# Score matmuls of a hybrid attention trunk: 128 rows with zeros in place of 64 rows

## The chip, the cores and the metric

The kernel runs on one core of one Trainium2 chip. The metric is device time in microseconds (us) of one execution; lower is better. Three runs of the kernel before gave 862.95, 865.4 and 859.62 us, a median of 862.95. The profile was taken in one further execution.

## The reference, cut to what matters

Two layers over 256 positions of width 1024. Each layer has a mixer with three branches (sliding-window attention, a gated short convolution, block attention), gated and merged, then a SwiGLU feed-forward part; each of the two is followed by a residual and a layer norm. With 256 positions and blocks of 256, the block attention is plain causal attention. Both attentions have 8 heads of 64 channels, and their scores are the part that the change touches:

```python
# sliding window (SWA), window 128, 8 query heads on 2 key heads, with sinks
logits = einsum('bnqhgd,bnkhd->bnhgqk', q, k) * 64 ** -0.5 - slope * dist
# block attention (MoBA), here the own block alone, 8 heads
lo = einsum('bhqd,bhkd->bhqk', q, kown) * 64 ** -0.5
lo = where(dist_own >= 0, lo - slope * dist_own, -inf)
```

All of it is float32. The kernel gets this precision on TensorE by splitting each operand in a high half (rounded to the matmul's format) and a low half (what is left): a product is high*high + high*low + low*high.

## The kernel before, in words

**The weights.** The weights come as a list of 140 pieces of 128 x 2048 floats, 70 for each layer, in the order in which they are used. `load` (L143) brings a piece into one of three raw buffers by SP's queue. `split_piece` (L187) cuts it in two chunks of 1024 columns: ScalarE writes the high half `wh` (L184), VectorE the low half `wl` (L185), into a ring of four slots. TensorE uses a piece in 48 matmuls of 256 columns (or their equal), two of them with `wh` and one with `wl` for each product. All matmuls but transposes and the mixing of values are issued by the helper `mm` (L255, so the trace has L256).

**The order of the work.** The program is unrolled and its order on each engine is written out when it is built: `Plan` (L52) keeps a model time of TensorE (`T.pe`), and tasks for ScalarE and VectorE are put in their queues when that time has passed their ready time. `mm` adds to the model time by the number of columns of the moving operand alone (L257, L103). Each engine then runs its own queue in order and waits on semaphores where it needs another's result.

**The attention.** Heads are taken in pairs, a pair being one round. A layer has eight rounds: four of SWA (`swa`, L653) and four of MoBA (`moba`, L658); in this text they are r0 to r7. Rounds are woven into the weight matmuls by `tick` (L223). A round goes through these steps:

- `prepare` (L404): for each head a of the pair, `me` is the 64 partitions of the head and `other` the other 64. The query tile `xq[:, a]` gets the query's high half on `me` and its low half on `other` (L409). The key tile `xk` is `kx` of L649, with two planes for each head: plane 0 has the key's high half on `me` and a copy of the key on `other` (L412), plane 1 has the key's low half on `me`. Before the first round of a layer GpSimd writes zeros to columns 0 to 127 of plane 1 on `other` (L651).
- `scores` (L449): for each head three matmuls into one PSUM tile `s` of four blocks of 128 columns. The first (L453) takes queries 128 to 255 on all 128 rows with plane 0: high*key_high plus low*key in one pass. The second (L454) adds high*key_low for the same queries, on the 64 rows of `me` alone. The third (L455) takes queries 0 to 127 with the first 128 keys of both planes at once, on all 128 rows, into blocks 0 and 3.
- `soft` (L419): VectorE adds the distances and takes the maximum (L444 to L426), ScalarE takes the exponential (L429, L431), VectorE scales (L439 to L441). The tile is `prob`.
- `turned` (L462): TensorE transposes `prob` into `tp` (L271), ScalarE copies it to `pt` (L280).
- `mixed` (L470): TensorE multiplies `pt` with the values into `yp` (L474, L476), and ScalarE and VectorE write the two halves of `y`.

The scores of the next round follow right behind the `yp` of this one. The tile `xa` that holds `xq` and `kx` shares its place in memory ("z") with the layer-norm constants `gb` of the part before.

**The convolution** runs beside rounds r1 to r4: its taps are on GpSimd (L714 to L717), between two products on VectorE (L283).

Of the kernel before, what the change touches and what calls it, by code (L numbers as in the profile page):

```python
# [9 lines left out]
FT = mybir.dt.float32  # L10
# [6 lines left out]
P = 128  # L17
D = 1024
S = 256
# [4 lines left out]
HD = 64  # L24
# [78 lines left out]
def pe_time(cols):  # L103
    return cols / 2400 + 0.0067


def dve(n):
    return "V", 0.07 + n * 0.00104
# [7 lines left out]
def trunk(ctx: ExitStack, tc: tile.TileContext, x, xt, w, sinks, conv, ln, out):  # L116
    nc = tc.nc
# [99 lines left out]
    def later(task, fn):  # L217
        waiting.append((task, fn))
# [27 lines left out]
    def bank(shape, tag, name):  # L246

        t = ps.tile(shape, FT, tag=tag, name=name)
        if len(banks[tag]) >= 4:
            for task in banks[tag].pop(0):  # L250
                T.finish(task)
        banks[tag].append([])
        return t, banks[tag][-1]

    def mm(acc, a, b, start, stop):  # L255
        nc.tensor.matmul(acc, a, b, start=start, stop=stop)  # L256
        T.pe += pe_time(int(np.prod(b.shape[1:])))  # L257
# [10 lines left out]
    def turn(src, n):  # L268
        tp, users = bank([P, n, P], "o", "tp")
        for i in range(n):  # L270
            nc.tensor.transpose(tp[:, i, :], src(i), ident)  # L271
            T.pe += pe_time(2 * P)
        return tp, users

    def halve(dst, src, n):
        return [act(n) + (lambda: nc.scalar.activation(dst[0], src, AF.Copy),),  # L276
                dve(n) + (lambda: nc.vector.tensor_sub(dst[1], src, dst[0].bitcast(FT)),)]  # L277

    def copy(dst, src, n):
        return [act(n) + (lambda: nc.scalar.activation(dst, src, AF.Copy),)]  # L280
# [16 lines left out]
    def after(users, ops, needs=(), **k):  # L297
        t = T.add(ops, needs=list(needs) + [had for _, _, had in claims if had], **k)
        for ring, i, _ in claims:
            ring[i] = t  # L300
        claims.clear()
        users.append(t)
        return t
# [3 lines left out]
    xk = [xx[:, k] for k in range(KD)]  # L307
# [107 lines left out]
    def attend(q, k, new_k, xq, xk, v, vsel, far, slopes, sink, dst, when):  # L415
        los = [slice(a * HD, (a + 1) * HD) for a in range(2)]
        pr, pts, tasks = [], [], []

        def soft(a, st, t, s):  # L419
            def top():  # L420
                nc.vector.tensor_reduce(st[:, 0:1], t[:, 0, :], axis=AX.X, op=OP.max)
                nc.vector.tensor_reduce(st[:, 1:2], t[:, 1:3, :], axis=AX.XY, op=OP.max)
                if sink is not None:
                    nc.vector.tensor_scalar(st[:, 2:4], st[:, 0:2], sink[1][a], -0.125, op0=OP.max, op1=OP.mult)
                else:
                    nc.vector.tensor_scalar_mul(st[:, 2:4], st[:, 0:2], -0.125)  # L426

            def power():
                nc.scalar.activation(t[:, 0, :], t[:, 0, :], AF.Exp, bias=st[:, 2:3], scale=0.125,  # L429
                                     accum_out=st[:, 4:5])  # L430
                nc.scalar.activation(t[:, 1:3, :], t[:, 1:3, :], AF.Exp, bias=st[:, 3:4], scale=0.125,  # L431
                                     accum_out=st[:, 5:6])
                if sink is not None:
                    nc.scalar.activation(st[:, 6:8], st[:, 2:4], AF.Exp, bias=sink[0][a], scale=1.0)

            def scale():
                if sink is not None:
                    nc.vector.tensor_add(st[:, 4:6], st[:, 4:6], st[:, 6:8])
                nc.vector.reciprocal(st[:, 6:8], st[:, 4:6])  # L439
                nc.vector.tensor_scalar_mul(t[:, 0, :], t[:, 0, :], st[:, 6:7])  # L440
                nc.vector.tensor_scalar_mul(t[:, 1:3, :], t[:, 1:3, :], st[:, 7:8])  # L441

            return [
                dve(384) + (lambda: nc.vector.scalar_tensor_tensor(t, far, -8.0 * slopes[a], s[:, 0:3, :],  # L444
                                                                   op0=OP.mult, op1=OP.add),),
                dve(P) + (lambda: nc.vector.tensor_add(t[:, 0, :], t[:, 0, :], s[:, 3, :]),),
                ("V", 0.75, top), ("A", 1.1, power), ("V", 0.9, scale)]

        def scores():  # L449
            ss = [bank([P, 4, P], "o", "s") for a in range(2)]  # L450
            for a in range(2):
                s, me = ss[a][0], los[a]
                mm(s[:, 1:3, :], xq[:, a, P:S], xk[:, a, 0, :], True, False)  # L453
                mm(s[:, 1:3, :], xq[me, a, P:S], xk[me, a, 1, :], False, True)  # L454
                mm(s[:, 0::3, :], xq[:, a, 0:P], xk[:, a, :, 0:P], True, True)  # L455
            for a in range(2):
                st = work.tile([P, 8], FT, name="st", bufs=4)
                pr.append(work.tile([P, 3, P], FT, tag="prob", name="prob", bufs=4))
                tasks.append(after(ss[a][1], soft(a, st, pr[a], ss[a][0])))
            later(tasks[-1], turned)  # L460

        def turned():  # L462
            T.finish(*tasks)
            for a in range(2):
                tp, users = turn(lambda i: pr[a][:, i, :], 3)
                pts.append(work.tile([P, 3, P], FT, name="pt"))
                tasks.append(after(users, copy(pts[a], tp, 384)))
            later(tasks[-1], mixed)

        def mixed():  # L470
            T.finish(*tasks)
            yp, users = bank([P, S], "o", "yp")
            for a in range(2):
                nc.tensor.matmul(yp[los[a], :], v[:, 0, vsel[a]], pts[a][:, 0:2, :], start=True, stop=False)  # L474
            for a in range(2):
                nc.tensor.matmul(yp[los[a], P:S], v[:, 1, vsel[a]], pts[a][:, 2, :], start=False, stop=True)  # L476
            T.pe += pe_time(4 * 384)
            at["y"].append(after(users, halve(dst, yp, S), due=8.0))
            busy[0] -= 1

        rounds.append(Round(when, q, k, new_k, xq, xk, scores))

    def residual(acc, users, r, stats):
# [150 lines left out]
    for l in range(L):  # L634
# [13 lines left out]
        xa = keep.tile([P, 6, S], FR, tag="z", name="xa")  # L648
        xq, kx = xa[:, 0:2], xa[:, 2:6].rearrange("p (a i) s -> p a i s", a=2)  # L649
        for a in range(2):  # L650
            nc.gpsimd.memset(kx[HD - a * HD:P - a * HD, a, 1, 0:P].bitcast(FT), 0.0)  # L651

        def swa(j):  # L653
            attend(aq[:, j, :], ak, j == 0, xq, kx, av, (slice(0, HD), slice(HD, P)), far_w, (slope(j), slope(j + 4)),
# [278 lines left out]
```

## Time and profile before

| | |
|---|---|
| median of 3 runs | 862.95 us (859.62 to 865.4) |
| the profiled execution's own time | 860.16 us |
| its span, first to last instruction | 858.4 us |
| mean granted clock of TensorE | 0.997 |
| TensorE busy | 844.8 us, 98% of the span |
| VectorE, ScalarE, GpSimd busy | 68%, 53%, 6% |
| moved by DMA | 155.16 MB, 181 GB/s over the span |

The span is 1.8 us shorter than the execution's own time; that rest lies around the program. PE is TensorE's matmuls, PEld its weight loads, DVE is VectorE, ACT is ScalarE, POOL is GpSimd, SP is the engine that issues most transfers. L256 is line 256 of the kernel before. A matmul's length in a row holds its way through the array, so that matmuls overlap in the rows; what one costs is seen from the start of one to the start of the next. In a row `out<-in` are the program's tile names, then come the shape of the weights (64*128 is 64 rows and 128 columns) and the shape of the moving operand.

### The profile page before, as it was taken

The numbers are of one execution on the slowest core, as the hardware profiler recorded it, in microseconds if no ns is written. First come the engines' busy times: TensorE is split into PE (matmuls) and PEld (weight loads), VectorE is DVE, ScalarE is ACT, GpSimd is POOL, SyncE is SP. The second block draws the span as 40 slices with busy tenths as digits, with TensorE's granted clock in tenths as the row PEclk, the third lists the DMA queues.
The fourth block names the chain that finished last, engine by engine and source line by source line (L and its number), as shares of the span: only waits on it lengthen the run. The fifth ranks groups of instructions, "written<-read, shape, count | busy, mean of one in ns | idle before, by whom it ended". The sixth has DMA issues, their size and how long they took to land.

```text
span 858.4 us, 15516 instructions
## 1 busy us (share of the span) xinstructions
PE 844.8 (98%) x6374; PEld 797.3 (93%) x6374; DVE 583.5 (68%) x977; ACT 456.3 (53%) x809; POOL 51.4 (6%) x81
## 2 busy tenths in 40 slices
PE   7999999999999999999999999999999999999996
PEld 7989999999899999988899899999997999999885
DVE  5678888567976666545656798876689575666435
ACT  6667577745535445434337757776564254444320
POOL 2003400000100000000000034000000000000000
PEclk9999999999999999999999999999999999999998
DMA  8754535365755555556337352544557465555511
GB/s 300 289 195 150 187 108 186 140 216 176 265 197 180 174 187 197 196 189 238 119 116 255 116 196 99 186 138 169 196 197 254 139 245 187 173 185 193 196 50 49
DMA packets 24822, 155.16 MB, mean 181 GB/s; under 512 B 2704, under 2 KB 4528, under 8 KB 7344
## 3 DMA queue, kind: packets, MB, share of 16 engines
q1 hardware_dynamic: 23536, 149.96, 49.9%
q0 software_dynamic: 1216, 4.22, 1.5%
q8 instruction: 50, 0.82, 0.4%
q14 instruction: 20, 0.16, 0.1%
HBM read 153.11 MB, written 1.05 MB: 180 GB/s over the span
## 4 chain that ended last, share of the span: by engine, by line
PE 96%; DMA 2%; DVE 1%; ACT 0%; issue 0%; SPq 0%; POOLq 0%; POOL 0%; DVEq 0%
PE acc L256 47%; PE pr L256 17%; PE hp L256 9%; PE br L256 8%; PE gc L256 5%; PE s L256 3%; PE cv L256 3%; PE tp L271 2%; DMA gb<-ln 1%; PE yp L474 1%; DMA xs<-xt 1%; PE yp L476 0%; DVE xtok L502 0%; DVE wA L185 0%; SPq L156 0%
## 5 line engine op out<-in xcount | busy, mean ns | idle before, releaser
L256 PE MATMUL acc<-xx,wh 128*128 128x256 f32 x2304 | 408.9, 282 | 5.6 <-ACT wh L276 5.6
L185 DVE TENSOR_TENSOR wl<-raw,wh 128x1024 fp32r<-128x1024 f32 x266 | 321.9, 1228 | 123.2 <-ACT wh L184 122.3
L184 ACT ACTIVATE wh<-raw 128x1024 fp32r<-128x1024 f32 x266 | 273.5, 1054 | 188.5 <-PE acc L256 81.6
L256 PEld LDWEIGHTS acc<-xx,wh 128*128 128x128 f32 x2304 | 353.9, 190 | 6.7 <-ACT wh L276 6.2
L256 PE MATMUL acc<-xx,wl 128*128 128x256 f32 x1152 | 323.2, 281 | 0.0
L256 PEld LDWEIGHTS acc<-xx,wl 128*128 128x128 f32 x1152 | 217.7, 189 | 0.2 <-DVE wl L277 0.2
L256 PE MATMUL hp<-wh,xx 128*128 128x256 f32 x384 | 70.5, 281 | 0.0
L283 DVE TENSOR_TENSOR g<-g,acc 128x256 f32<-128x256 f32 x72 | 30.1, 417 | 58.7 <-PE acc L256 58.7
L256 PE MATMUL br<-y,wh 128*128 128x256 f32 x384 | 67.9, 281 | 0.0
L256 PE MATMUL pr<-wh,hidA 128*128 128x512 f32 (+1 forms) x216 | 60.8, 366 | 0.0
L256 PEld LDWEIGHTS hp<-wh,xx 128*128 128x128 f32 x384 | 59.5, 188 | 0.0
L256 PEld LDWEIGHTS br<-y,wh 128*128 128x128 f32 x384 | 59.0, 190 | 0.0
L256 PE MATMUL br<-y,wl 128*128 128x256 f32 x192 | 54.0, 281 | 0.0
L256 PE MATMUL hp<-wl,xx 128*128 128x256 f32 x192 | 53.5, 279 | 0.0
L256 PE MATMUL gc<-xx,wh 128*128 128x256 f32 x256 | 45.3, 281 | 0.0
L256 PEld LDWEIGHTS pr<-wh,hidA 128*128 128x128 f32 x216 | 39.1, 189 | 6.7
L256 PE MATMUL pr<-wh,hidB 128*128 128x512 f32 (+1 forms) x144 | 41.8, 366 | 0.0
L256 PE MATMUL pr<-wl,hidA 128*128 128x512 f32 (+1 forms) x108 | 39.6, 366 | 0.0
L256 PEld LDWEIGHTS gc<-xx,wh 128*128 128x128 f32 x256 | 39.3, 190 | 0.0
L429 ACT ACTIVATE prob<-prob,st 128x128 f32<-128x128 f32 x32 | 12.6, 395 | 46.3 <-DVE st L426 23.3
L256 PEld LDWEIGHTS hp<-wl,xx 128*128 128x128 f32 x192 | 36.1, 188 | 0.0
L256 PEld LDWEIGHTS br<-y,wl 128*128 128x128 f32 x192 | 36.0, 188 | 0.0
(130 smaller groups left out, 982.0 us busy)
## 6 DMA issues: line engine op xcount, KB each, us to landing
raw<-w SPq DMA_DIRECT2D x136, 1024.0 KB, 4.9
gb<-ln POOLq DMA_DIRECT2D x8, 512.0 KB, 5.9
raw<-w SPq DMA_DIRECT2D x6, 512.0 KB, 6.5
xtok<-x SPq DMA_DIRECT2D x2, 512.0 KB, 6.3
xs<-xt SPq DMA_DIRECT2D x3, 256.0 KB, 5.4
raw<-w SPq DMA_DIRECT2D x3, 256.0 KB, 5.5
out<-xtok SPq DMA_DIRECT2D x3, 256.0 KB, 2.0
xs<-xt SPq DMA_DIRECT2D x2, 128.0 KB, 2.5
```

Source lines behind the costliest of these rows:

```text
L184: return [act(n) + (lambda: nc.scalar.activation(wh[:, s], raw[j][:, s], AF.Copy),), dve(n) + (lambda: nc.vector.tensor_sub(wl[:, s], raw[ ...
L185: dve(n) + (lambda: nc.vector.tensor_sub(wl[:, s], raw[j][:, s], wh[:, s].bitcast(FT)),)]
L256: nc.tensor.matmul(acc, a, b, start=start, stop=stop)
L271: nc.tensor.transpose(tp[:, i, :], src(i), ident)
L283: return [dve(n) + (lambda: nc.vector.tensor_mul(dst, a, b),)]
L429: nc.scalar.activation(t[:, 0, :], t[:, 0, :], AF.Exp, bias=st[:, 2:3], scale=0.125, accum_out=st[:, 4:5])
L474: nc.tensor.matmul(yp[los[a], :], v[:, 0, vsel[a]], pts[a][:, 0:2, :], start=True, stop=False)
```

## The change

The second score matmul takes all 128 rows of `xq` and of plane 1 in place of the 64 rows of `me`. On the rows of `other` plane 1 has to be zero for all 256 columns, so the memset writes 256 columns in place of 128. Nothing else differs.

```diff
@@ -449,9 +449,9 @@
         def scores():
             ss = [bank([P, 4, P], "o", "s") for a in range(2)]
             for a in range(2):
-                s, me = ss[a][0], los[a]
+                s = ss[a][0]
                 mm(s[:, 1:3, :], xq[:, a, P:S], xk[:, a, 0, :], True, False)
-                mm(s[:, 1:3, :], xq[me, a, P:S], xk[me, a, 1, :], False, True)
+                mm(s[:, 1:3, :], xq[:, a, P:S], xk[:, a, 1, :], False, True)
                 mm(s[:, 0::3, :], xq[:, a, 0:P], xk[:, a, :, 0:P], True, True)
@@ -648,7 +648,7 @@
         for a in range(2):
-            nc.gpsimd.memset(kx[HD - a * HD:P - a * HD, a, 1, 0:P].bitcast(FT), 0.0)
+            nc.gpsimd.memset(kx[HD - a * HD:P - a * HD, a, 1, :].bitcast(FT), 0.0)
```

## Rows read from the trace of the kernel before

**Rows 1.** The page: busy times of the engines, TensorE's clock in 40 slices.
```profile
PE 844.8 (98%) x6374; PEld 797.3 (93%) x6374; DVE 583.5 (68%) x977; ACT 456.3 (53%) x809; POOL 51.4 (6%) x81
...
PEclk9999999999999999999999999999999999999998
```

**Rows 2.** The page: the chain that ended last, by engine.
```profile
PE 96%; DMA 2%; DVE 1%; ACT 0%; issue 0%; SPq 0%; POOLq 0%; POOL 0%; DVEq 0%
```

**Rows 3.** Waits of TensorE's matmuls: us in total, times, longest.
```profile
PE acc L256 <- ACT wh L276: 5.6, 3, 4.7
PE tp L271 <- DVE xtok L502: 0.7, 1, 0.7
```

**Rows 4.** Timeline, TensorE, round r0: start, length; each row begins one matmul later.
```profile
46.35 0.28 PE L256 MATMUL s<-xa 128*128 128x256 f32 x1
...
46.56 0.69 PE L256 MATMUL s<-xa 64*128 64x256 f32 x2
...
46.87 0.50 PE L256 MATMUL s<-xa 128*128 128x256 f32 x2
...
47.09 0.59 PE L256 MATMUL s<-xa 128*128 128x256 f32 x2
...
47.83 0.28 PE L256 MATMUL acc<-xx,wh 128*128 128x256 f32 x1
```

**Rows 5.** Timeline, TensorE's weight loads, the same round.
```profile
46.56 0.18 PEld L256 LDWEIGHTS s<-xa 64*128 64x128 f32 x1
...
46.98 0.19 PEld L256 LDWEIGHTS s<-xa 128*128 128x128 f32 x1
```

**Rows 6.** Timeline, TensorE, round r1: its six score matmuls and what follows them.
```profile
60.39 1.75 PE L256 MATMUL s<-xa 128*128 128x256 f32 x6
61.98 0.40 PE L256 MATMUL cv<-wh,xx 128*128 128x512 f32 x1
```

**Rows 7.** The chain in order of time: start, us, what.
```profile
76.24 8.18 PE acc L256 x72
...
428.99 8.48 PE hp L256 x72
```

**Rows 8.** Groups by shape: count, then busy us and mean ns of one.
```profile
L256 PE MATMUL s<-xa 64*128 64x256 f32 x32 | 12.1, 380 | 0.0
```

**Rows 9.** Stretches r3, r4: us; busy PE, PEld, DVE, ACT, POOL; clock, DMA, GB/s.
```profile
88.54:102.90 14.36, 14.36 (x119) 13.40 (x117) 13.32 (x30) 9.86 (x25) 5.02 (x4) 1.00 0.46 165
102.90:117.06 14.16, 14.16 (x119) 13.35 (x117) 10.93 (x28) 9.26 (x24) 5.18 (x7) 1.00 0.32 123
```

**Rows 10.** Timeline, VectorE: the softmax of r2 (second head), r3, r4, r5 begins.
```profile
76.27 0.56 DVE L444 SCALAR_TENSOR_TENSOR prob<-far_w,s 128x384 f32<-128x384 f32 x1 [0.19 <-PE s L256]
...
89.81 1.07 DVE L444 SCALAR_TENSOR_TENSOR prob<-far_w,s 128x384 f32<-128x384 f32 x2
...
106.21 1.00 DVE L444 SCALAR_TENSOR_TENSOR prob<-far_c,s 128x384 f32<-128x384 f32 x2
...
119.73 1.01 DVE L444 SCALAR_TENSOR_TENSOR prob<-far_c,s 128x384 f32<-128x384 f32 x2
```

**Rows 11.** Timelines, ScalarE's `pt` and TensorE's `yp` in r4, then in r5.
```profile
115.36 0.85 ACT L280 ACTIVATE pt<-tp 128x384 f32<-128x384 f32 x2
...
116.15 0.76 PE L474 MATMUL yp<-pt,mix 128*64 128x256 f32 x4
...
128.77 0.86 ACT L280 ACTIVATE pt<-tp 128x384 f32<-128x384 f32 x2
...
130.30 0.65 PE L474 MATMUL yp<-pt,mix 128*64 128x256 f32 x4
```

**Rows 12.** Timeline, GpSimd: memsets of layer 0 (one of two), layer 1.
```profile
12.55 0.20 POOL L651 MEMSET xa<- 64x128 f32 x1 [7.85 <-DMA raw<-w]
...
435.64 0.45 POOL L651 MEMSET xa<- 64x128 f32 x2 [1.69 <-DVE xtok L502]
```

**Rows 13.** The span's end, TensorE: us, busy, granted clock, DMA share, GB/s.
```profile
850.00:858.40 8.40, 1.07 (x9) 0.71 0.17 62
```

## The prediction

> **What bounds the kernel now.** I read the page first. TensorE is busy for 98% of the span at the full clock [rows 1], and 96% of the chain that ended last runs through it [rows 2]. A busy TensorE may still stand still between matmuls, so the next view is its waits: 6.3 us in all, at the first weights and at one layer norm, and none at scores, transposes or `yp` [rows 3]. So the time is TensorE's own sequence, and what a matmul of it costs is the distance of starts in the timeline.
>
> In ordinary stretches that is 8.18 / 72 = 0.114 us for a matmul of 256 columns, and 8.48 / 72 = 0.118 us where the moving operand is two blocks of 128 apart from each other, as in `hp` [rows 7]. Now the scores of round r0 [rows 4]: from the first (128 rows) to the second (64 rows) 0.21 us, from the second to the third 0.31, from the third to the next head's first 0.22; the second head repeats it and the six take 47.83 - 46.35 = 1.48 us. Six ordinary ones would take 4 x 0.114 + 2 x 0.118 = 0.69.
>
> The weight loads say why [rows 5]. In an ordinary stretch the load for the next matmul runs beside the matmul before. The load of the 64-row matmul begins only at 46.56, with the matmul itself, and that of the third begins with its matmul too, at 46.87; the fourth's begins at 46.98, ahead of its matmul at 47.09. So TensorE lets the array run empty (0.21 - 0.11 = 0.10 us) when it goes from 128 rows to 64 and again on the way back (0.10), and each time it then has a load that nothing hides (0.11 in the second's 0.31, 0.11 in the third's 0.22): 0.4 us a head.
>
> **The change part by part.**
>
> *The second matmul gets 128 rows* (32 of them [rows 8]). The columns stay at 256, so its own work stays at 0.114. Both switches of height go. In r0 the saving is 1.48 - 0.69 = 0.79 us. In the other rounds the scores follow `yp`, whose weights are 64 columns wide; the first score then has a load of its own that nothing hides, and the six take 61.98 - 60.39 = 1.59 us [rows 6]. That load stays: 0.69 + 0.11 = 0.80, and the saving is 0.79 again. Sixteen rounds give 12.6 us on TensorE.
>
> The third matmul is the one term that no row settles alone: its output goes to two blocks apart from each other, and part of its 0.22 could be that. If all of it were, 0.22 - 0.118 = 0.10 would stay for each head, 32 x 0.10 = 3.3 us, and the gain of TensorE is 9.3. The other end is 12.6. I take 12.6, since the fourth's load begins a plain 0.11 after the third's start [rows 5], and the distance is then that of a load and a matmul in line.
>
> The Trainium skill speaks against the change at one place ("TensorE: Matmul & The Clock Gate", Part 3: Packing small matmuls): matmuls on different row groups of the array run at the same time, so that a half-height one beside another costs a few ns, which full height gives up. By that rule a 64-row matmul would be nearly free and each of the 32 new ones would cost 0.114 more, 3.6 us. Here the trace does not agree: the two heads' 64-row matmuls have two full ones between them, and each has 0.31 us to itself.
>
> *The waits.* The second matmul now reads the low half of the queries, the whole of plane 1 and so the memset. The first one already waits for all of `xq`, and the third for the zeros in columns 0 to 127. Nothing new is late. One more semaphore wait could be set on the second; at 0 if it is met, as the waits of the other scores are. Behind it stands TensorE's whole queue, and the softmax waits for it; but the zeros would have to be over 30 us late to hold it (next paragraph).
>
> *The memset* doubles its columns: 0.20 us becomes 0.20 to 0.40 (an estimate, at most double), twice in each layer. On GpSimd's queue it stands ahead of `far_w` and the sinks in layer 0, at 12.55, with nothing that needs them before 47.6; in layer 1 at 435.6 with the scores at 467 [rows 12]. Cover of over 30 us: 0. No transfer is added or moved.
>
> *The order* of all queues stays, since the model time counts columns alone.
>
> *What is late next.* TensorE comes 0.79 us earlier at each round, and this is worth something only if VectorE and ScalarE follow. They feed it twice a round: `prob` for the transposes, `pt` for `yp`. Up to r2 VectorE waits for the scores, so it follows (the second softmax of r2 waits 0.19 us for TensorE [rows 10]). From then on it doesn't: in r3 VectorE is busy for 13.32 of 14.36 us [rows 9]. The start of a softmax lies 89.81 - 88.54 = 1.27 us behind the scores in r3, 3.31 in r4, 2.67 in r5 [rows 9, 10]. So r4 is where VectorE is furthest behind already, and there `pt` is done at 115.36 + 0.85 = 116.21, when `yp` has just begun at 116.15 (its second head needs the second `pt`): no room is left [rows 11].
>
> So I follow VectorE through it. It is moved by r2's scores, the third round: its two softmaxes come 2.0 and 2.4 us earlier, in line 2.2 to 2.4; I take 2.3. From there to r4's `pt` it and ScalarE work without leaning on TensorE, and r4's `pt` is done 2.3 us earlier. TensorE would be at r4's `yp` after five rounds of scores, 5 x 0.79 = 3.95 earlier. It has to wait about 3.95 - 2.35 = 1.6 us there. In r5 `pt` ends at 129.63, 0.67 before `yp` [rows 11]; VectorE's round from r4 to r5 takes 13.52 us and TensorE's new one 14.16 - 0.79 = 13.37, so it can't catch up, and TensorE is 2.35 + 0.79 = 3.14 earlier against 2.3: that uses up the room of r5 and asks for 0.1 us at the most. For r6 and r7 I take r5's room as the measure. Behind the wait three rounds still give 3 x 0.79 = 2.37.
>
> Sum for a layer: 2.35 + 2.37 = 4.7 us; layer 1 has the same order. Two layers: 9.4 us, of the 12.6 that TensorE saves; 3.2 are given back at r4.
>
> Against the profiled execution: 860.16 - 9.4 = 850.8 us. That execution lies 2.8 us under the median of the runs (862.95) and near their lowest; by the median it is 853.5. I predict between the two, 852.0.
>
> **The rivals.**
>
> *The others keep up.* VectorE and ScalarE follow TensorE wholly (their queues hold splits of weights that could be done sooner), no wait shows at r4, and all 12.6 us come through: 847.5 by the profile, 850.3 by the median. For it: the chain has 0% of either engine now [rows 2]. Against it: 13.32 of 14.36 us busy, and queues that run in order.
>
> *The third matmul keeps its 0.22*: 0.59 us a round. Five rounds are 2.95, VectorE moves by about 1.7, so 1.2 are given back a layer, and the gain is 2 x (8 x 0.59 - 1.2) = 7.0: 853.1 by the profile, 855.9 by the median. Against it stands the place of the loads.
>
> *The change doesn't do what it says*: the 0.21 and 0.31 come not from the height but from a matmul that adds to what the one before has just written, or from the semaphores on these loads. Then nothing changes, 863. Against it: `acc` and `hp` add to one tile at 0.114 throughout.
>
> *Half-height matmuls were nearly free.* If a 64-row matmul ran beside its neighbours and the distances of r0 belonged to something else that stays, each full-height one would add 0.114 us, 32 x 0.114 = 3.6: 863.8. Against it: the second score has 0.31 us to itself [rows 4]. This is what the Trainium skill's rule above would do here.
>
> *Slower, by the clock.* The wait at r4's `yp` is the one place where the change makes TensorE stand still. At the end of the span, where TensorE is busy for 1.07 of 8.4 us, its granted clock is 0.71 on the mean, so it falls towards its lower level (1.2 of 2.4 GHz) when TensorE is idle [rows 13]. If the wait of 1.6 us did that, the matmuls behind it would take twice as long until it rose again. The gain is gone when 4.7 us of matmul work a layer run at the lower level; with 10 us of it the time is 850.8 + 20 = 871. Against it: the clock is at full in every slice before the end [rows 1].
>
> **How the numbers follow.** Forecast (gain partly given back at r4) 0.57; others keep up 0.22; third matmul keeps its cost 0.12; nothing saved 0.06; half-height ones free 0.01; slower by the clock 0.02. The range goes from 846 (all 12.6 against the profile's own time, less 1.5 for a run as low as the lowest shown) to 857 (the third matmul's case by the median, and 1 more): what it leaves out is the case with nothing saved, the free half-height matmuls, the clock, and the edges of the others. What a measurement can tell from no change is about 1%, 8.6 us. My forecast of 9.4 is just over it: I give two thirds of its chance to faster, all of "keep up" and a tenth of the third matmul's: 0.38 + 0.22 + 0.01 = 0.61. Slower by over 1% is the clock's 0.02, and within 1% the rest, 0.37.
>
> **What would show it.** No weight load of 64 rows is left. Starts of the second and third score 0.11 to 0.12 after the one before; the six in 0.80 behind `yp` and 0.69 in r0 and its like in layer 1. A score group with 64 rows gone and 96 of 128. If the third still takes 0.22, that term was wrong. In r4 of each layer a wait of TensorE for ScalarE's `pt` of 1 to 2 us, and the rounds r5 to r7 shorter by 0.79. If no wait for `pt` shows, the give-back was wrong; if the waits show at the transposes, I had the wrong place. The prediction is wrong as a whole if the six scores still take 1.5 us, or if the stretch r0 to r7 is shorter by 0.79 x 8 and the time is not.

## The result, and the profile after

The kernel after took 853.75 us in the median of 4 runs (852.73 to 855.76), the kernel before 864.17 in the median of 4 (859.62 to 866.96). The ratio on record is 0.991, with a 95% interval from 0.9887 to 0.9932; the quotient of these two medians is 0.988, just below that interval. So the gain is 7.8 us by the ratio and 10.4 by the medians. The forecast was 852.0 in a range from 846 to 857. The profiled execution of the kernel after took 852.73 us with a span of 851.0, against 860.16 and 858.4 before: 7.4 us between the two profiles, where the forecast's sum was 9.4.

First the score matmuls. The groups by shape of the kernel after (count, then busy us and mean ns of one) and TensorE's timeline of rounds r0 and r1 answer to [rows 8], [rows 4] and [rows 6]:

```profile
L256 PE MATMUL s<-xa 128*128 128x256 f32 x96 | 15.4, 296 | 0.0
...
46.83 0.87 PE L256 MATMUL s<-xa 128*128 128x256 f32 x6
47.53 0.40 PE L256 MATMUL acc<-xx,wh 128*128 128x256 f32 x2
...
60.08 0.98 PE L256 MATMUL s<-xa 128*128 128x256 f32 x6
60.90 0.39 PE L256 MATMUL cv<-wh,xx 128*128 128x512 f32 x1
```

No 64-row form is left. The six scores take 47.53 - 46.83 = 0.70 us in r0 and 60.90 - 60.08 = 0.82 in r1, where it was 1.48 and 1.59. Added up over the 16 rounds, the distances of starts come to 12.8 us in place of 25.2: TensorE's own saving is 12.4 us, and the forecast had 12.6.

Now what TensorE waits for, in the kernel after (us in total, times, longest), against [rows 3]:

```profile
PE acc L256 <- ACT wh L276: 4.9, 2, 4.4
PE yp L474 <- ACT pt L280: 3.2, 3, 1.5
PE tp L271 <- DVE xtok L502: 0.9, 1, 0.9
PE acc L256 <- DVE wl L185: 0.7, 1, 0.7
```

The second row is new: `yp` waits for ScalarE's `pt`. The timelines of round r4 show where, ScalarE's row first, then TensorE's; they answer to the first pair of [rows 11]:

```profile
114.15 0.85 ACT L280 ACTIVATE pt<-tp 128x384 f32<-128x384 f32 x2
...
112.86 0.28 PE L256 MATMUL acc<-xx,wl 128*128 128x256 f32 x1
114.67 0.81 PE L474 MATMUL yp<-pt,mix 128*64 128x256 f32 x3 [1.54 <-ACT pt L280]
```

In the kernel before, the last matmul ahead of the `yp` at 116.15 was this:

```profile
115.94 0.28 PE L256 MATMUL acc<-xx,wl 128*128 128x256 f32 x1
```

After the change the last matmul ahead begins at 112.86 and `yp` at 114.67; before, that distance was 116.15 - 115.94 = 0.21 us. So the wait that came with the change is 1.81 - 0.21 = 1.60 us; in layer 1 it is 1.73 - 0.21 = 1.52. The stretch of r4 is longer than before although its scores are shorter: 15.41 us in the windows of the kernel after, against 14.16 in [rows 9] (columns as there).

```profile
86.67:100.44 13.77, 13.72 (x118) 13.06 (x116) 12.81 (x31) 10.46 (x26) 3.76 (x3) 1.00 0.46 159
100.44:115.85 15.41, 13.87 (x118) 13.08 (x117) 12.18 (x29) 9.37 (x25) 6.35 (x8) 1.00 0.35 129
```

To see what becomes of the saving I take the stretch of a layer from its first score to its first `br`, in which nothing but rounds and their weight matmuls lies, and add up TensorE's distances from start to start by what the matmul is (the one ahead of a round's transposes is counted with them). In us, for layer 0 and layer 1:

| part of the stretch | before | after | difference |
|---|---|---|---|
| scores | 12.60, 12.60 | 6.42, 6.41 | -6.2, -6.2 |
| last matmul ahead of `yp`, to `yp` | 1.77, 1.77 | 3.49, 3.53 | +1.7, +1.8 |
| `yp` | 6.51, 6.52 | 7.40, 7.41 | +0.9, +0.9 |
| transposes | 5.63, 5.63 | 5.77, 5.77 | +0.1, +0.1 |
| weight matmuls (`acc`, `cv`) | 89.59, 89.59 | 88.96, 89.05 | -0.6, -0.5 |
| all | 116.10, 116.10 | 112.04, 112.16 | -4.1, -3.9 |

So 6.2 us a layer are saved, 2.8 given back at `yp` and the transposes, and 0.6 come from somewhere that the forecast did not have (the pace of TensorE, below). By rounds, the 2.8 of layer 0 are 2.0 in r4 (1.60 ahead of `yp`, 0.28 within it, 0.14 at the transposes), 0.5 in r3 and 0.25 in r5 and r6.

Within `yp` the two heads part. In the kernel before the first matmul of the second head starts 0.01 us after that of the first in r3; in the kernel after it starts 0.38 us after it in r3 and in r4, since its own `pt` is not there, and `yp` takes 1.18 us in place of 0.80 and 0.90.

The two layers gain 8.0; ahead of the first score the kernel after happened to be 0.5 us later (46.83 against 46.35), and that leaves the 7.4 of the profiles.

### The profile page after: what moved, and what is told of

It is laid out like the page before. It is cut to its first block, busy times and chain, and to the rows that moved or that the text cites. A ratio compares the mean times of both kernels' runs of the same rounds, so it can differ in the third digit from the quotient of the medians.

```text
span 851.0 us, 15520 instructions
## 1 busy us (share of the span) xinstructions
PE 834.0 (98%) x6374; PEld 793.2 (93%) x6374; DVE 584.0 (69%) x977; ACT 455.8 (54%) x809; POOL 52.0 (6%) x81
## 4 chain that ended last, share of the span: by engine, by line
PE 88%; DVE 4%; ACT 3%; DMA 2%; POOL 2%; issue 1%; SPq 1%; POOLq 0%; DVEq 0%; ACTq 0%
PE acc L256 41%; PE pr L256 18%; PE hp L256 9%; PE br L256 8%; PE gc L256 5%; PE cv L256 3%; PE tp L271 2%; PE s L256 1%; DMA gb<-ln 1%; PE yp L474 1%; DMA raw<-w 1%; DVE wl L185 1%; ACT wh L184 1%; POOL hh L716 1%; POOL t L717 1%
## 5 line engine op out<-in xcount | busy, mean ns | idle before, releaser
L429 ACT ACTIVATE prob<-prob,st 128x128 f32<-128x128 f32 x32 | 12.6, 395 | 45.3 <-DVE st L426 23.3
```

## The experiments

All ran against the kernel before on the same chip; a ratio is the estimate on record from all runs of both kernels, with its 95% interval, and lies within 0.002 of the quotient of their medians. A trace shows one execution alone. The totals carry two things that have nothing to do with the change. The first score began between 46.2 and 48.4 us in the ten profiles of this study, and the wait of the first matmuls behind a layer norm for its constants (`tp` for `xtok`) was 0.7 to 4.6 us. So the stretch above is read beside each ratio.

### Two half-height matmuls side by side

The kernel before, with the order of the six scores changed:

```diff
-            for a in range(2):
-                s, me = ss[a][0], los[a]
-                mm(s[:, 1:3, :], xq[:, a, P:S], xk[:, a, 0, :], True, False)
-                mm(s[:, 1:3, :], xq[me, a, P:S], xk[me, a, 1, :], False, True)
-                mm(s[:, 0::3, :], xq[:, a, 0:P], xk[:, a, :, 0:P], True, True)
+            for a in range(2):
+                mm(ss[a][0][:, 1:3, :], xq[:, a, P:S], xk[:, a, 0, :], True, False)
+            for a in range(2):
+                me = los[a]
+                mm(ss[a][0][:, 1:3, :], xq[me, a, P:S], xk[me, a, 1, :], False, True)
+            for a in range(2):
+                mm(ss[a][0][:, 0::3, :], xq[:, a, 0:P], xk[:, a, :, 0:P], True, True)
```

> The kernel before with its score matmuls in another order: both heads' first ones, then both heads' 64-row ones side by side (they lie on different rows of the array), then both heads' third ones. Height theory (each change of height lets the array run empty, 0.10 us, and leaves one load uncovered, 0.11): two changes a round in place of four, the six scores of r0 take about 1.09 us in place of 1.48, 16 x 0.39 = 6.3 us saved on TensorE, some of it given back at r4, 4 to 5 us in all. Rival A (the distance comes from adding to what the matmul just before has written): the 64-row ones no longer follow the matmul that wrote their tile, all distances become 0.11 to 0.12, and the six take 0.7. Rival B (two half-height matmuls on different rows run at the same time): the distance from the first 64-row one to the second is a few hundredths of a us and the six take 0.95 or less.

Ratio 0.9946 (0.9926 to 0.9965). TensorE's timeline of r0, cut so that rows begin with the half-height pair and with the third score, its weight load between them:

```profile
48.05 1.14 PE L256 MATMUL s<-xa 128*128 128x256 f32 x6
...
48.38 0.39 PE L256 MATMUL s<-xa 64*128 64x256 f32 x2
...
48.69 0.19 PEld L256 LDWEIGHTS s<-xa 128*128 128x128 f32 x1
...
48.69 0.38 PE L256 MATMUL s<-xa 128*128 128x256 f32 x1
...
49.03 0.40 PE L256 MATMUL acc<-xx,wh 128*128 128x256 f32 x2
```

The six take 49.03 - 48.05 = 0.98 us. The two half-height matmuls together cover 0.39 us, where one alone covers 0.38: they start 3 to 4 ns apart in all 16 rounds. Ahead of them stands the 0.21 of a change to 64 rows and behind them the 0.31 back, once a round now. Rival A falls, since no score here follows the matmul that wrote its tile, and the 0.21 and 0.31 are there all the same: they belong to the height. The kernel after says so from the other side: there the second score follows the one that wrote its tile and starts 0.12 us behind it. The height theory holds for the changes and had the pair wrong, which rival B had right but for a size: 0.98 where it said 0.95 or less.

This is what the Trainium skill says ("TensorE: Matmul & The Clock Gate", Part 3): matmuls on different row groups run together. The trace agrees as soon as the two are neighbours, with 3 to 4 ns between them; in the kernel before they are not, and each cost as much as the pair. What such a pair pays is in the Trainium skill as well, without a number ("TensorEngine Tiling (Array Packing)", Key Properties: a change of mode drains the array). Here it is 0.10 us for each change, and a load of 0.11 that nothing covers behind it; the rows show this delay and not what happens in the array.

The stretch falls to 113.5 and 113.8 us. The waits at `yp` of r4 are there (2.8 us in two layers), though the saving is 4.0 a layer and not 6.2.

### The change in r5 to r7 alone, and in r0 to r4 alone

The kernel after, with the rows chosen by round:

```diff
-                mm(s[:, 1:3, :], xq[:, a, P:S], xk[:, a, 1, :], False, True)
+                on = slice(0, P) if full else los[a]
+                mm(s[:, 1:3, :], xq[on, a, P:S], xk[on, a, 1, :], False, True)
```

with `full` handed in as a new argument, false in `swa` and `j > 0` in `moba` for the late rounds, true in `swa` and `j == 0` in `moba` for the early ones.

> The kernel after with the second score on 128 rows in rounds r5 to r7 alone, on 64 rows in r0 to r4. Theory (the give-back is the wait at r4's yp, because VectorE, GpSimd and ScalarE up to there do not follow TensorE): nothing is given back, no wait for pt at r4, and 2 layers x 3 rounds x 0.77 = 4.6 us come through. Rival (the give-back is spread over all rounds, a share of each): of the 7.9 us that the attention stretches gained, 3/8 come through, 3.0 us.

> The kernel after with the second score on 128 rows in rounds r0 to r4 alone, on 64 rows in r5 to r7: the other half of the run with late rounds alone. Theory (what is given back is given back at r3 and r4): TensorE's scores shorten by 5 x 0.77 = 3.9 us a layer, the wait at r4's yp is there with about 1.7 us, and of the 3.9 about 1.5 to 2 come through in the stretch from the first score to the first br, which was 116.1 us before. Rival (a like share of each round is given back): 5/8 of what the kernel after gained there net of TensorE's pace, 5/8 x 3.4 = 2.1, and the wait is smaller, about 1.

Late rounds alone: ratio 0.9895 (0.9876 to 0.9913). Early rounds alone: 0.9956 (0.9941 to 0.9972). What TensorE waits for, late first, then early:

```profile
PE acc L256 <- ACT wh L276: 5.3, 2, 4.4
PE tp L271 <- DVE xtok L503: 4.6, 2, 4.0
```

```profile
PE acc L256 <- ACT wh L276: 4.7, 2, 4.4
PE yp L475 <- ACT pt L280: 3.2, 3, 1.5
PE tp L271 <- DVE xtok L503: 1.2, 2, 0.8
```

With the late rounds alone there is no wait for `pt`. The scores of a layer are 2.3 us shorter, the stretch is 113.75 against 116.1: all of the saving comes through (0.3 us lost within `yp` and 0.3 won by weight matmuls cancel). With the early ones alone the scores are 3.9 us shorter, the wait for `pt` is the whole 3.2 us of the kernel after, and the stretch is 114.5 and 114.9: only 1.6 and 1.2 come through. The forecast for this run was 1.5 to 2, so layer 1 lies under it; the rival's 2.1, with a wait of about 1, is farther off. So the give-back is made by the scores of r0 to r4 and paid at r3 and r4, for the most part at r4, and not by each round for itself.

One thing did not fit. The late rounds should have gained 4.6 us in all, and the ratio says 9. The chain in order of time shows a difference behind the stretch; the kernel after first, then late rounds alone:

```profile
159.03 33.92 PE br L256 x288
192.95 22.61 PE gc L256 x192
```

```profile
160.16 32.64 PE br L256 x288
192.80 21.77 PE gc L256 x192
```

The same 480 matmuls take 56.53 us in one and 54.41 in the other, 0.1178 and 0.1133 us each, in both layers. 2 x 2.1 = 4.2 us of the gain in this profile have nothing to do with scores. But the same execution lost 3.7 us again behind a layer norm (waits of 4.6 in place of 0.9), and at 856.54 us it was the slowest of six, with a median of 853.46. What the five others did no trace shows, so it is likely but not shown that the pace makes up the 9. A run on the pace comes below.

### What sets r4's `pt`

Three kernels on this. In the first the taps 1 and 2 of the convolution are left out of the kernel after, so GpSimd does one operation of five for each group, and the order on the other engines stays:

```diff
                     nc.gpsimd.tensor_mul(z, up[:, i, 0:S], tap[0])
-                    for n in (1, 2):
-                        nc.gpsimd.tensor_mul(other, up[:, i, n:S + n], tap[n])
-                        nc.gpsimd.tensor_add(z, z, other)
```

> The kernel after with the convolution's taps 1 and 2 left out (one product on GpSimd in place of five operations for each of four groups); the order on all other engines is the same. Theory (in r4 the softmax stands behind a product on VectorE that waits for these taps, so GpSimd's length sets when pt is ready): the wait at r4's yp falls from 1.7 us to 0.4 or less in each layer, 2.5 to 3 us faster than the kernel after. Rival A (ScalarE's own queue, where pt stands behind a split of weights): the wait stays at 1.3 to 1.7. Rival B (VectorE is full with splits and softmax whatever GpSimd does): it stays at over 1.

Ratio 0.9868 (0.9846 to 0.989); the profiled execution was the fastest of six (847.11, median 852.4), so the stretch is what counts. There is no wait for `pt`, the part ahead of `yp` is 1.77 us as in the kernel before, and the stretch is 109.18 us in both layers, 2.9 and 3.0 less than after. Rounds r3 and r4 run at TensorE's own pace:

```profile
86.25:99.53 13.28, 13.28 (x118) 12.84 (x116) 11.98 (x30) 9.84 (x24) 3.02 (x2) 1.00 0.39 139
99.53:112.81 13.28, 13.28 (x118) 12.84 (x116) 10.97 (x29) 9.93 (x25) 0.00 (x0) 1.00 0.38 147
```

Both rivals fall: ScalarE's queue has the same order and `pt` behind the same split, and VectorE has the same instructions, though they take less time (11.98 us busy in r3 in place of 12.81). The rows of the kernel after show the path. First GpSimd in r3 and r4, then VectorE:

```profile
98.03 1.59 POOL L716 TENSOR_TENSOR hh<-mix,cw 128x256 f32<-128x256 f32 x1
99.70 1.59 POOL L717 TENSOR_TENSOR t<-t,hh 128x256 f32<-128x256 f32 x1
...
104.19 0.61 POOL L716 TENSOR_TENSOR hh<-mix,cw 128x256 f32<-128x256 f32 x1
```

```profile
97.93 1.23 DVE L185 TENSOR_TENSOR wl<-raw,wh 128x1024 fp32r<-128x1024 f32 x1
...
100.62 1.75 DVE L185 TENSOR_TENSOR wl<-raw,wh 128x1024 fp32r<-128x1024 f32 x1
...
103.70 0.42 DVE L283 TENSOR_TENSOR t<-t,acc 128x256 f32<-128x256 f32 x1 [1.32 <-POOL t L717]
...
105.01 1.01 DVE L444 SCALAR_TENSOR_TENSOR prob<-far_c,s 128x384 f32<-128x384 f32 x2
```

The same product in the kernel before:

```profile
104.90 0.42 DVE L283 TENSOR_TENSOR t<-t,acc 128x256 f32<-128x256 f32 x1 [1.31 <-POOL t L717]
```

VectorE's product at 103.70 has waited 1.32 us for the taps, and r4's softmax stands behind it in the queue. The taps are late because they run beside splits: the same operation takes 1.59 us beside them and 0.61 with no split beside it, and a split 1.75 in place of 1.23. VectorE's wait is not new: in the kernel before it was 1.31 us for the same taps. What is new is that TensorE now comes to `yp` before `pt` is done. The Trainium skill ("GPSIMD Engine Reference", Specifications) has GpSimd's SBUF interfaces shared with VectorE where an instruction reads two SBUF operands; a split does, and the trace agrees as far as these lengths go.

The taps work on r4's `pt` in a second way. Counted from the first score of layer 0, r2's two softmaxes begin 1.7 and 2.0 us earlier than in the kernel before, r3's 1.5 and 1.6, r4's 1.7. With the short taps it is 1.7 and 2.0, then 2.7 and 2.8, then 4.9. So between r2 and r3, beside the taps of the first two groups, VectorE loses about 0.5 us of what it had gained, and with short taps it gains 0.7 there. The wait of 1.3 us and the slower split ahead of r4's softmax come on top.

The control is the kernel before with the same two taps left out:

> The kernel before, with the convolution's taps 1 and 2 left out. Control for the run with fewer taps on the kernel after: there the stretch from the first score to the first br fell by 2.9 us. Theory (the taps cost time only because TensorE comes earlier now): in the kernel before they are hidden, and the stretch stays at 116.1 us less 0.1 for the small wait at r4's yp, apart from the pace. Rival (shorter taps save time in either kernel): it falls by 1 us or more.

Ratio 1.0025 (1.0008 to 1.0042), stretch 116.30 us in both layers, with `yp` 0.1 us shorter and the weight matmuls 0.3 longer. In the kernel before the taps hold VectorE but not TensorE, and the time gains nothing without them; only with the change does TensorE feel them. The total is 2 us longer, the two stretches together only 0.4; in its profile the wait behind a layer norm was 2.7 us in place of 0.7.

Then two attempts to give r4 its time back with all the work done. In one the plan's cost of the taps is raised from 4.0 to 7.0 (L719), which puts the product that waits for them behind most of r4's softmax:

> The kernel after with the taps' cost in the plan at 7.0 in place of 4.0, so that the product that waits for them stands behind most of r4's softmax in VectorE's queue. The order of TensorE is the same. Theory as for the run with fewer taps: the wait at r4's yp falls below 0.5 us, 2 to 3 us faster than the kernel after. Rival A (ScalarE's queue): no change, within 0.5 us. Rival C: the products of the convolution are now late for what reads them, and the wait only moves to a later place; the time stays within 1 us of the kernel after.

Ratio 0.9909 (0.9888 to 0.9929). The part ahead of `yp` falls from 3.5 to 2.3 us, but `yp` rises from 7.4 to 8.1 and 7.9, and the stretch is 111.7 and 111.2. The wait at r4 has gone for the most part, and waits in r2, r3, r5 and r6 have come, so rival C was the nearest, though not by its mechanism. In the other the last scaling of the SWA softmax goes from VectorE to ScalarE:

```diff
-                ("V", 0.75, top), ("A", 1.1, power), ("V", 0.9, scale)]
+                ("V", 0.75, top), ("A", 1.1, power)] + (
+                [("V", 0.9, scale)] if sink is None else [("V", 0.4, scale), ("A", 0.7, spread_a)])
```

where `spread_a` does the two products of L440 and L441 as ScalarE copies with a scale.

> The kernel after with the last scaling of the SWA rounds (two products a head) on ScalarE in place of VectorE, so VectorE has 1.3 us less in each of r0 to r3 and the taps and r4's softmax can begin earlier. Theory (VectorE and GpSimd in r2 to r4 are what r4's yp waits for): the wait at r4's yp falls from 1.7 us to below 0.5 and the stretch from the first score to the first br falls from 112.1 us to 109.5 to 110.5. Rival (the taps on GpSimd alone set it, whatever VectorE has to do): the wait stays at 1.3 or more. Second rival: ScalarE is now late, a wait for prob shows at the transposes of r1 to r3 and nothing is gained.

Ratio 0.9907 (0.9888 to 0.9927). The timeline of r4's `yp`:

```profile
112.86 0.28 PE L256 MATMUL acc<-xx,wl 128*128 128x256 f32 x1
113.72 0.65 PE L483 MATMUL yp<-pt,mix 128*64 128x256 f32 x2 [0.58 <-ACT pt L280]
```

The distance falls from 1.81 to 0.86 us and the stretch to 110.9 in both layers, 1.1 and 1.3 less than after. It is short of what was expected (0.5 and 109.5 to 110.5), and both rivals fall: VectorE's work in r0 to r3 is part of the cause, beside the taps, or reaches r4 through the time at which they begin; the run does not tell these apart. In the total it does not show: its ratio lies on that of the kernel after, and in its profile 2.5 us more went into the wait behind a layer norm (3.4 against 0.9). Of the kernels that do all of the work none was measurably faster than the kernel after.

### The two paces of TensorE

The kernel after with one transpose more behind the last `yp` of a layer:

```diff
             busy[0] -= 1
+            if not rounds:
+                turn(lambda i: pr[0][:, i, :], 1)
```

> The kernel after with one transpose more (one block of prob into a free PSUM tile that nothing reads) behind the last yp of each layer. In all kernels but the one with late rounds alone the 412 matmuls behind that yp went at 0.1178 us each, in that one at 0.1133. Theory (TensorE has two steady paces, and the event behind which a stretch begins decides which; behind transposes it is the fast one): from there to the first layer norm each matmul takes 0.1133, about 1.9 us less a layer, 3.8 us in all, against 0.1 to 0.2 for the transpose. Rival (the pace belongs to the matmuls of that stretch, and the one fast run had another cause): the pace stays at 0.1178 and the time is that of the kernel after, plus 0.3.

Ratio 0.9922 (0.9893 to 0.9952). In layer 0 `br` took 32.64 us, in layer 1 33.92: one layer went over to the fast pace and one did not. The pace is not tied to these matmuls, then, but a transpose ahead does not decide it either, and what does is open. In layer 0 the 2.1 us were lost again: the wait behind the layer norm was 3.1 us there, since the later half of the constants `gb` was issued 2.6 us earlier than in the kernel after but took 11.9 us to land in place of 8.4.

## Why the prediction was right, and where it was off

*The cost of a change of height.* This term held. It was read from the starts and the loads, 0.79 us a round; 0.77 was measured, with 0.70 and 0.82 for the six scores against 0.69 and 0.80. The run with the pairs shows that it was the height and not the tile that is added to. The case in which the third matmul keeps its 0.22 fell: it takes 0.12.

*The waits, the memset, the order.* Costed at nothing, and nothing of them shows: the order on the four engines is the same, the memsets are 64 x 256 (0.31 us each in place of 0.20), and no score waits for them.

*The give-back at r4.* This step made the forecast, and it was there: the place, the instruction waited for and both layers. The term that was off is its size. I had 1.6 us a layer at r4 and at most 0.1 later; 2.75 were measured (+1.7 ahead of `yp`, +0.9 within it, +0.1 at the transposes). The step that failed is "It is moved by r2's scores" and the 2.3 us that VectorE was to come earlier. In the kernel after neither softmax of r2 waits for TensorE: they begin 1.7 and 2.0 us earlier, and r4's begins, counted from the layer's first score, at 105.01 - 46.83 = 58.18 us in place of 106.21 - 46.35 = 59.86: 1.7 earlier. And I looked for its cause in VectorE's own load; the runs show the taps on GpSimd, beside which VectorE's instructions take longer and for which it then waits, with VectorE's load as a part of it (1.1 to 1.3 us a layer came back when some of it went to ScalarE, 2.9 with short taps). For r3, whose second `pt` comes too late for `yp` to run as one, the forecast had no term; it is 0.5 us.

*The case in which the others keep up* fell by the wait that showed. *The clock:* a wait of 1.5 us left the granted clock at 1.00 in r4's window, so the slower case did not come. *The half-height matmuls that run for free* are real, as the run with the pairs shows, but only side by side; the trace of the kernel before, where they are apart, did not speak against the rule.

*What came by luck:* 0.6 us a layer by the pace of weight matmuls made up for half of what the give-back was sized too small. The total of 4.0 a layer, where 4.7 was forecast, is therefore nearer than its parts. The wait at r4 itself, forecast at 1.6 and measured at 1.60 and 1.52, is luck too: `pt` was 0.6 us later than forecast, and TensorE was held up at r3 before it came to r4. And 852.0 lay near the measured median also because it was put between two bases that differ by 2.8 us.

## What to carry to other kernels

A matmul on half of the rows between two on all rows is dear here: it takes 0.50 us of TensorE where one on all rows takes 0.12 (0.77 us a round were saved on two of them), since each change of height delays by 0.10 and leaves a load of 0.11 without cover. Fill it up with zeros, or put half-height ones on different rows side by side, where two cost what one does; in this kernel the zeros were the better of the two, 0.70 us for the six scores in place of 0.98. And when the engine that bounds a kernel gets faster, look in its timeline for the place where the others already arrive last: most of what is given back is paid there, and not spread over the rounds (2.0 of 2.8 us in r4).

## What the runs showed of the hardware that was not expected

TensorE has two steady paces for the same matmuls of 128 x 128 with 256 columns, 0.1133 and 0.1178 us, at the same granted clock of 1.00. It holds one for a whole stretch (480 matmuls in `br` and `gc`). In the ten traces none of the 240 unbroken rows of 48 or more of these matmuls goes over from one to the other; the pace changes where the row is broken, at scores, `yp` or transposes, and which of the two follows is open. The 0.118 of `hp` in [rows 7], which the forecast put down to its moving operand in two blocks, is this second pace as well: `br`, with plain operands, has it too, and `hp` itself took 8.16 us for 72 matmuls early in the kernel before. In the profile with late rounds alone it is worth 4.2 us, over half of the 7.4 between the profiles before and after.
